# Context mixer and routing ahead of the latent stream's filters, in a two-layer hybrid diffusion kernel

## The chip, the cores and the metric

The kernel runs on one core of one Trainium2 chip. The metric is device microseconds (us) of one execution, lower is better. Its engines here are TensorE (PE in the rows), VectorE (DVE), ScalarE (ACT), GpSimd (POOL) and SyncE (SP), which issues the plain transfers. Each engine works through one list of instructions that is fixed when the kernel is built.

## The reference

Two layers work on 512 latent tokens of width 1024 and on 256 context tokens. In short form:

```
for l in range(2):
    mod_x, mod_c = silu(c) @ w_mod[l] + b_mod[l], silu(c_ctx) @ w_mod[l] + b_mod[l]   # 6 parts each
    hx, hc = rmsnorm(x)*(1+sc1)+sh1, rmsnorm(ctx)*(1+csc1)+csh1
    yx, yc = token_mixer(hx, hc)          # RG-LRU | latent attention | Hyena, one w_in before, one w_out behind
    x   = x + g1*yx
    x   = x + g2*peer(rmsnorm(x)*(1+sc2)+sh2)
    if l == 0:
        ctx = ctx + cg1*yc
        ctx = ctx + cg2*peer(rmsnorm(ctx)*(1+csc2)+csh2)
return rmsnorm(x)

def peer(h):                               # 8 heads, 16 of 128*128 experts per head and token
    s1, s2 = scores of the two halves of h @ wq against 128 keys each
    eid, gate = the 16 best sums of pairs, softmax of their scores
    return sum over the 128 (gate * gelu(h . u_tab[eid])) * v_tab[eid]
```

The Hyena convolution needs the spectra of its filters, which come from a small network (the filters) and depend on the layer's weights and the length alone, not on the tokens. The latent stream needs the context's keys, values and recurrent end state in each layer.

## The kernel before

All arithmetic is fp32; the large products are three fp32r passes over a high and a low part (`split` makes them, L113 on ACT and L114 on DVE; `mm` at L121 multiplies).

`peer` is done in two ways. For most latent tokens the tables are streamed whole, 128 blocks of `u` and of `v` (tiles `uv`, `uvh`, `uvl`, products `pst` and `dacc`; function `peer_x`). For the 256 context tokens and the last 128 latent tokens of layer 0 the rows are gathered: `gtile_u` and `gtile_v` take a tile of 128 tokens and issue 128 indirect transfers each, one row of a table per token (L1097 on POOL, tile `grow`, five buffers, 512 KB per transfer). Behind each gather stands one DVE instruction that uses it (L1108 for `u`, L1121 for `v`). Layer 0 has six such passes, 768 gathers; layer 1 has 384.

What sets the order: `schedule` is written with levels (`prio`). A lower level goes ahead, and an instruction of a higher level is put into the lists where the planner sees room. The gathers have level 6, the last. The context part has level 1, the latent mixer of layer 0 level 3. A pool gives its memory back when it closes, and what opens there afterwards waits for its tiles.

Before the change, one block at level 1 holds, in this order: the filters of the context length, the modulation's parts 0 and 1, the context's `front` (w_in, convolutions, Hyena, RG-LRU), the latent stream's filters of layer 0 (`filters`, L331 to L407), the modulation's parts 2 to 5, the context's `back` (attention, w_out), the latent stream's filters of layer 1, and parts 0 and 1 of layer 1's modulation. All its pools close there. Then comes the context's `route` (`ppq` for h @ wq, `top16` on DVE, `experts` for `eid`), still at level 1. The latent mixer's `front` of layer 0 opens its pools behind the block and not behind the routing, so that it can stand among the routing's instructions. Its products are `pwin` of 128x512 (`split=False`: 288 matmuls). The gathers of the first context tile can begin when the first half of `eid` (L1068) is there.

SP's list is in order as well: it holds the loads of the filters' transforms (`ffr`, `ffi`, L394 and L395, two buffers each), of the modulation's weights (`wmod`, L264), of `w_in`, of the routing's weights (`wpq`, L294) and others.

Of the kernel before, what the change touches and what calls it, by code (L numbers as in the profile page):

```python
# [23 lines left out]
LC = 256  # L24
# [47 lines left out]
class Kern:  # L72
# [100 lines left out]
    def schedule(self):  # L173
        a = self.a
        with ExitStack() as er:
            ec = ExitStack()
            self.context(ec, 0)
            with self.banks("ctx0", "right", w=2, S=1) as ps, ExitStack() as e0:
                md = e0.enter_context(self.pool("mod", side="right"))
                pm = e0.enter_context(self.banks("mod", "right", w=1))  # L180
                fl = e0.enter_context(self.pool("flt"))
                pf = e0.enter_context(self.banks("flt", "left", w=2, S=1))
                with self.prio(1), ExitStack() as e:
                    self.filters(fl, pf, 0, LC)
                    self.modulation(md, pm, 0, 0, 2)
                    st = self.front(e, ps, ps, 0, 1, 1, side="right")
                    self.filters(fl, pf, 0, LX)
                    self.modulation(md, pm, 0, 2, 6)
                    self.back(ps, ps, 0, 1, st, None)
                    self.filters(fl, pf, 1, LX)  # L190
                    self.modulation(md, pm, 1, 0, 2)
            self.gp = er.enter_context(self.pool("gath", side="right"))
            with self.prio(1), self.banks("rc", "right", w=2) as ps:
                gc = self.route(ps, 0, 1, "GG", side="right")
            with self.banks("x0", "left", w=2, S=2) as ps:
                with ExitStack() as e:
                    with self.prio(3):
                        pr = e.enter_context(self.banks("x0b", "right", w=2))
                        st = self.front(e, ps, pr, 0, 0, 3, split=False)
                        ex = ExitStack()  # L200
                        self.back(ps, pr, 0, 0, st, ex)
                ec.close()
            with self.prio(6):
                self.gtile_u(0, gc[0])
                self.gtile_v(0, 1, 0, gc[0])
                self.gtile_u(0, gc[1])
            with self.prio(3):
                gx, ex = self.peer_x(0, 384, 6, 32, 32, (36, 46, 46), ex)
            with self.prio(6):
                self.gtile_u(0, gx[3])  # L210
                self.gtile_v(0, 0, 3, gx[3])
                self.gtile_v(0, 1, 1, gc[1])
            with ExitStack() as ec, ExitStack() as e:
                self.context(ec, 1)
                ps = e.enter_context(self.banks("x1", "left", w=2, S=2))
                pr = e.enter_context(self.banks("x1b", "right", w=2))
                with self.prio(3):
                    st = self.front(e, ps, pr, 1, 0, 4, ctx=True)
                with self.prio(4):
                    self.back(ps, pr, 1, 0, st, None, (2, 6))  # L220
            with self.prio(5):
                gx, _ = self.peer_x(1, 320, 0, 32, 46, (44, 42, 42), ex)
            with self.prio(6):
                for i in sorted(gx, reverse=True):
                    self.gtile_u(1, gx[i])
                    self.gtile_v(1, 0, i, gx[i])
# [1211 lines left out]
```

## Time and profile before

| what | us |
|---|---|
| three runs | 4273.55, 4275.73, 4280.51 (median 4275.73) |
| the profiled execution | 4275.16 |
| its span, first to last instruction | 4273.3 |
| PE, DVE, ACT, POOL busy in it | 3707.9, 3510.8, 1904.1, 1532.1 |

The span falls into stages. Up to 318 us runs the context mixer with the filters; at 374 the first `ppq` product of its routing starts; the routing's last `eid` is there at about 531; the latent mixer's Hyena starts at about 605; at 893 the latent stream's own routing begins, with the dense `u` blocks beside it; from 1230 to 2461 the dense blocks run; at 2500 layer 1's mixer is under way. Layer 1 takes the rest. A row with a window gives, after the window and its length, each engine's busy time and in brackets its instructions, then the granted TensorE clock as a share of 2.4 GHz, the share of the 16 DMA engines that is busy, and GB/s.

### The profile page before, as it was taken

To read this page: it belongs to the slowest core of one execution; us is meant where nothing else is said; L and a number is where in the kernel's file an instruction comes from. 1 tells how busy PE (TensorE), PEld (TensorE's weight loads), DVE (VectorE), ACT (ScalarE), POOL (GpSimd) and SP (SyncE) were. 2 spreads that over 40 slices of the span, in tenths; PEclk is the share of its full clock that TensorE was granted. 3 is DMA by queue.
4 is the path that set the end of the run, shared out by engine and by line. 5 is a ranking of instruction groups with operands and counts; after the bars stand their busy time and mean duration, and the time that the engine had idled before them with its cause. 6 is when DMAs were issued, how large, how long until landed. Compare 5 with 4: busy or idle time off the path is not lost.

```text
span 4273.3 us, 63792 instructions
## 1 busy us (share of the span) xinstructions
PE 3707.9 (87%) x22514; PEld 2805.8 (66%) x22514; DVE 3510.8 (82%) x7449; ACT 1904.1 (45%) x3719; POOL 1532.1 (36%) x1225
## 2 busy tenths in 40 slices
PE   6887987968978989999969978888888999999997
PEld 3545544558878877877646656447878877776654
DVE  5746988889889889988898875755898998898988
ACT  5544243433257426622552244533334655555632
POOL 0000245642344563366436620000126345553243
PEclk7998998988999999999989989898999999999998
DMA  6654587885767897799879952242459788887697
GB/s 208 211 192 157 202 304 252 286 299 187 257 224 258 311 348 254 249 359 352 286 233 346 342 190 82 92 134 100 136 180 352 265 300 299 287 302 277 226 349 269
DMA packets 305635, 1063.74 MB, mean 249 GB/s; under 512 B 35757, under 2 KB 42625, under 8 KB 305315
## 3 DMA queue, kind: packets, MB, share of 16 engines
q0 software_dynamic: 165888, 604.05, 40.6%
q1 hardware_dynamic: 139426, 455.61, 30.6%
q8 instruction: 177, 2.90, 0.3%
q14 instruction: 144, 1.17, 0.1%
HBM read 1042.69 MB, written 16.84 MB: 248 GB/s over the span
## 4 chain that ended last, share of the span: by engine, by line
PE 32%; DMA 22%; DVE 17%; issue 16%; POOL 7%; ACT 5%; SPq 0%; POOLq 0%; DVEq 0%; ACTq 0%
PE pst L121 7%; POOL grow L1097 7%; DMA grow<-in_peer_v_dram,eid 6%; PE dacc L121 6%; DMA grow<-in_peer_u_dram,eid 6%; DMA uv<-in_peer_ut_dram 4%; PE pwin L121 4%; PE ppq L121 3%; DMA uv<-in_peer_v_dram 3%; DVE uvl L114 3%; DVE acc L1108 2%; DVE acc L1121 2%; PE pwo L121 2%; DMA wmod<-in_w_mod_dram 1%; ACT uvh L113 1%
## 5 line engine op out<-in xcount | busy, mean ns | idle before, releaser
L1097 POOL DMA_INDIRECT grow<-in_peer_u_dram,eid x576 | 747.8, 1298 | 1157.3 <-DVE acc L1108 566.4
L1097 POOL DMA_INDIRECT grow<-in_peer_v_dram,eid x576 | 776.6, 1348 | 746.4 <-DVE acc L1121 601.0
L121 PE MATMUL pst<-dhT,uvh 128*128 128x384 f32 (+1 forms) x4096 | 1001.6, 329 | 0.0
L113 ACT CAST uvh<-uv 128x1024 fp32r<-128x1024 f32 x491 | 513.0, 1045 | 680.5 <-DMA uv<-in_peer_v_dram 411.3
L121 PE MATMUL pst<-dhT,uvl 128*128 128x384 f32 (+1 forms) x2048 | 696.8, 340 | 112.3 <-DVE uvl L114 77.2
L1121 DVE SCALAR_TENSOR_TENSOR acc<-grow,gate,acc 128x1024 f32<-128x1024 f32 x571 | 732.2, 1282 | 53.8 <-DMA grow<-in_peer_v_dram,eid 46.0
L1108 DVE SCALAR_TENSOR_TENSOR acc<-grow,ghx 128x1024 f32<-128x1024 f32 x576 | 704.1, 1222 | 75.3 <-DMA grow<-in_peer_u_dram,eid 68.1
L121 PEld LDWEIGHTS pst<-dhT,uvh 128*128 128x128 f32 x4096 | 733.0, 193 | 4.1 <-issue 1.9
L114 DVE TENSOR_TENSOR uvl<-uv,uvh 128x1024 fp32r<-128x1024 f32 x491 | 599.1, 1222 | 159.5 <-ACT uvh L113 152.9
L121 PEld LDWEIGHTS pst<-dhT,uvl 128*128 128x128 f32 x2048 | 395.8, 193 | 212.3 <-DVE uvl L114 155.5
L121 PE MATMUL dacc<-uvh,wl 128*128 128x512 f32 x1154 | 481.2, 417 | 38.4 <-DVE wl L114 19.1
L121 PE MATMUL dacc<-uvl,wh 128*128 128x512 f32 x1154 | 467.3, 405 | 25.2 <-DVE uvl L114 25.1
L121 PE MATMUL dacc<-uvh,wh 128*128 128x512 f32 x1154 | 462.8, 401 | 0.0
L1235 ACT ACTIVATE o<-iota,di2n 128x128 f16<-128x128 f32 x1056 | 325.6, 390 | 28.8 <-PE pwt L1239 28.5
L121 PEld LDWEIGHTS dacc<-uvh,wl 128*128 128x128 f32 x1154 | 220.3, 191 | 128.4 <-ACT uvh L113 30.6
L121 PEld LDWEIGHTS dacc<-uvl,wh 128*128 128x128 f32 x1154 | 220.6, 191 | 82.7 <-DVE uvl L114 38.3
L121 PEld LDWEIGHTS dacc<-uvh,wh 128*128 128x128 f32 x1154 | 220.8, 191 | 48.3
L1239 PEld LDWEIGHTS <-o 128*128 128x128 f16 x4224 | 126.1, 97 | 110.7 <-issue 32.7
L1239 PE MATMUL pwt<-og,o 128*128 128x46 f16 (+3 forms) x4224 | 152.0, 182 | 43.3 <-DVE og L1225 35.5
L1205 ACT ACTIVATE PA<-pst 128x384 f32<-128x384 f32 (+1 forms) x128 | 59.5, 464 | 281.0 <-PE pst L121 280.9
L1205 ACT ACTIVATE PB<-pst 128x384 f32<-128x384 f32 (+1 forms) x128 | 59.2, 462 | 232.4 <-PE pst L121 231.8
L254 POOL MEMSET rmod<- 128x512 f32 (+1 forms) x8 | 3.3, 417 | 420.3 <-PE lpg L722 99.7
(399 smaller groups left out, 6092.6 us busy)
## 6 DMA issues: line engine op xcount, KB each, us to landing
uv<-in_peer_ut_dram SPq DMA_DIRECT2D x256, 512.0 KB
uv<-in_peer_v_dram SPq DMA_DIRECT2D x256, 512.0 KB
wmod<-in_w_mod_dram SPq DMA_DIRECT2D x96, 512.0 KB
wpq<-in_peer_wq_dram SPq DMA_DIRECT2D x48, 512.0 KB
w_in<-in_w_in_dram SPq DMA_DIRECT2D x72, 256.0 KB
w_in<-in_w_in_dram SPq DMA_DIRECT2D x18, 512.0 KB
grow<-in_peer_u_dram,eid POOLq DMA_INDIRECT x576
grow<-in_peer_v_dram,eid POOLq DMA_INDIRECT x576
```

The costliest lines, as they stand in the source:

```text
L113: self.nc.scalar.copy(hi, src)
L114: self.nc.vector.tensor_tensor(lo, src, hi.bitcast(F32), op=ALU.subtract)
L121: self.nc.tensor.matmul(p, w[i], x[j], start=start and n == 0, stop=stop and n == len(passes) - 1)
L254: nc.gpsimd.memset(r, 0.0)
L1097: self.nc.gpsimd.indirect_dma_start(out=r, out_offset=None, in_=self.a[table], in_offset=bass.IndirectOffsetOnAxis(ap=eid[:, j:j + 1], axi ...
L1108: nc.vector.scalar_tensor_tensor(junk, r, 1.0, hx, op0=ALU.mult, op1=ALU.mult, accum_out=dot[:, j:j + 1])
L1121: nc.vector.scalar_tensor_tensor(acc, r, w[:, j:j + 1], acc, op0=ALU.mult, op1=ALU.add)
L1205: nc.scalar.activation(slot(i), p, AF.Gelu_apprx_tanh)
L1235: nc.scalar.activation(o2[:, q], self.iota, AF.Abs, bias=i2n[:, t, k * NC + q:k * NC + q + 1])
L1239: nc.tensor.matmul(p[:, q, :], o2[:, q, :], og[:, g, q, :], start=(g == 0), stop=(g == 1))
```

## The change

The modulation's and the filters' pools now stand outside, on the left side, and stay open through the routing. The latent stream's filters of both layers and layer 1's modulation move behind the routing in the text and go down to level 2; the context's `back` and `route` stay at level 1. The gather's pool (`gath`) opens inside. The latent mixer's pools open when the filters' pools have closed, so behind the routing and the filters. Lines below L200 keep their numbers; those behind are 2 higher after the change.

```diff
-            with self.banks("ctx0", "right", w=2, S=1) as ps, ExitStack() as e0:
-                md = e0.enter_context(self.pool("mod", side="right"))
-                pm = e0.enter_context(self.banks("mod", "right", w=1))
+            with ExitStack() as e0:
+                md = e0.enter_context(self.pool("mod"))
+                pm = e0.enter_context(self.banks("mod", w=1))
                 fl = e0.enter_context(self.pool("flt"))
                 pf = e0.enter_context(self.banks("flt", "left", w=2, S=1))
-                with self.prio(1), ExitStack() as e:
-                    self.filters(fl, pf, 0, LC)
-                    self.modulation(md, pm, 0, 0, 2)
-                    st = self.front(e, ps, ps, 0, 1, 1, side="right")
+                with self.prio(1):
+                    with self.banks("ctx0", "right", w=2, S=1) as ps, ExitStack() as e:
+                        self.filters(fl, pf, 0, LC)
+                        self.modulation(md, pm, 0, 0, 2)
+                        st = self.front(e, ps, ps, 0, 1, 1, side="right")
+                        self.modulation(md, pm, 0, 2, 6)
+                        self.back(ps, ps, 0, 1, st, None)
+                    self.gp = er.enter_context(self.pool("gath", side="right"))
+                    with self.banks("rc", "right", w=2) as ps:
+                        gc = self.route(ps, 0, 1, "GG", side="right")
+                with self.prio(2):
                     self.filters(fl, pf, 0, LX)
-                    self.modulation(md, pm, 0, 2, 6)
-                    self.back(ps, ps, 0, 1, st, None)
                     self.filters(fl, pf, 1, LX)
                     self.modulation(md, pm, 1, 0, 2)
-            self.gp = er.enter_context(self.pool("gath", side="right"))
-            with self.prio(1), self.banks("rc", "right", w=2) as ps:
-                gc = self.route(ps, 0, 1, "GG", side="right")
```

What it does to the lists is seen at three places. The first is POOL's list before the change, over the second half of the latent mixer's `front` of layer 0 (`upad` is the padded input of a convolution, `grow` a gather):

```order
L507 MEMSET upad 128x1
L508 MEMSET upad 128x1
L1097 DMA grow<-in_peer_u_dram,eid 128x1024 x5
L492 MEMSET upad 128x2
L493 MEMSET upad 128x1
L1097 DMA grow<-in_peer_u_dram,eid 128x1024 x3
L492 MEMSET upad 128x2
L493 MEMSET upad 128x1
L1097 DMA grow<-in_peer_u_dram,eid 128x1024 x7
L492 MEMSET upad 128x2
L493 MEMSET upad 128x1
L1097 DMA grow<-in_peer_u_dram,eid 128x1024 x104
```

With 9 ahead of the first row, 24 gathers stand ahead of the last `upad`. The same list after the change, from its first gather on:

```order
L1099 DMA grow<-in_peer_u_dram,eid 128x1024 x36
L509 MEMSET upad 128x1
L510 MEMSET upad 128x1
L509 MEMSET upad 128x1
L510 MEMSET upad 128x1
L1099 DMA grow<-in_peer_u_dram,eid 128x1024 x24
L509 MEMSET upad 128x1
L510 MEMSET upad 128x1
L1099 DMA grow<-in_peer_u_dram,eid 128x1024 x4
L509 MEMSET upad 128x1
L510 MEMSET upad 128x1
L1099 DMA grow<-in_peer_u_dram,eid 128x1024 x5
```

Four groups of 4, 4, 5 and 5 follow between the other `upad`s, so that 87 gathers stand ahead of the last one, and the first 36 ahead of the first.

The second place is DVE's list where the context's routing ends. Before, the last `eid` stands among the latent convolutions (`xx`) and the start of its RG-LRU (`sp`):

```order
L555 SCALAR_TENSOR_TENSOR xx_4398<-upad,cols,xx_4398 128x512
L553 TENSOR_SCALAR xx_4399<-upad,cols 128x512
L1108 SCALAR_TENSOR_TENSOR acc,dot<-grow,ghx 128x1024
L1068 TENSOR_SCALAR eid<-pkb 128x64
L555 SCALAR_TENSOR_TENSOR xx_4399<-upad,cols,xx_4399 128x512
L685 TENSOR_SCALAR sp_5096<-cols 128x6
L703 TENSOR_SCALAR sphb<-cols 128x6
```

After the change the last `eid` (L1070) is followed by the second half of layer 1's filters (`frs`, `fkt`, `fks`), with one gather's instruction (L1110) between them each time, and the first latent norm (`xn`) stands 60 rows further down:

```order
L1070 TENSOR_SCALAR eid<-pkb 128x64
L373 TENSOR_TENSOR fsq<-fsq 128x512
L687 TENSOR_SCALAR sp_5096<-cols 128x6
L705 TENSOR_SCALAR sphb<-cols 128x6 x2
L688 TENSOR_TENSOR sp_5092<-cols,sp_5096 128x6
L1110 SCALAR_TENSOR_TENSOR acc,dot<-grow,ghx 128x1024
L690 TENSOR_SCALAR sp_5093<-sp_5092 128x6
L1110 SCALAR_TENSOR_TENSOR acc,dot<-grow,ghx 128x1024
L691 RECIPROCAL sp_5093<-sp_5093 128x6
L1110 SCALAR_TENSOR_TENSOR acc,dot<-grow,ghx 128x1024
L377 RECIPROCAL frs<-frs 128x512
L692 TENSOR_TENSOR sp_5093<-sp_5093,sp_5092 128x6
```

So the latent `front` no longer overlaps the routing; the filters do.

The third place is DVE's list at the end of layer 0 (`dacc` is the dense sum, `xs` the new latent tokens). Before, gathers of `v` go on past it:

```order
L114 TENSOR_TENSOR uvl<-uv,uvh 128x1024
L1121 SCALAR_TENSOR_TENSOR acc<-grow,gate,acc 128x1024 x3
L1304 TENSOR_TENSOR PA<-dacc_10704,PA 128x1024
L1304 TENSOR_TENSOR PA<-dacc_10705,PA 128x1024
L1146 TENSOR_TENSOR xs<-PA 128x1024 x2
L1304 TENSOR_TENSOR PA<-dacc_10706,PA 128x1024
L1121 SCALAR_TENSOR_TENSOR acc<-grow,gate,acc 128x1024
L1146 TENSOR_TENSOR xs<-PA 128x1024
L1121 SCALAR_TENSOR_TENSOR acc<-grow,gate,acc 128x1024
```

After, none is left there:

```order
L114 TENSOR_TENSOR uvl<-uv,uvh 128x1024
L1306 TENSOR_TENSOR PA<-dacc_10704,PA 128x1024
L1306 TENSOR_TENSOR PA<-dacc_10705,PA 128x1024
L1148 TENSOR_TENSOR xs<-PA 128x1024 x2
L1306 TENSOR_TENSOR PA<-dacc_10706,PA 128x1024
L1148 TENSOR_TENSOR xs<-PA 128x1024
L105 TENSOR_SCALAR nrm<-nss 128x1 x2
```

Counted over DVE's whole list, the gathers that stand ahead of five marks of layer 0 are, before and after: the routing's last `eid` 20 and 16; the latent Hyena's first product 56 and 132; the split of the latent stream's normed tokens (`dhT`) 179 and 255; the first weights of the dense part (L1220) 267 and 353; the first dense sum (L1304) 749 and 768. Between the last two marks the gathers stand equally dense against the dense blocks (`uvl`) in both lists, up to block 213 of 235; the last 22 blocks have 64 gathers before and none after.

## Rows read from the trace of the kernel before

**Rows 1.** The page: the span, and the chain that ended last by engine.

```profile
span 4273.3 us, 63792 instructions
...
PE 32%; DMA 22%; DVE 17%; issue 16%; POOL 7%; ACT 5%; SPq 0%; POOLq 0%; DVEq 0%; ACTq 0%
```

**Rows 2.** Windows by stage: length, busy us (instructions) per engine, clock, DMA.

```profile
0.00:318.00 318.00, 255.67 (x1429) 147.94 (x1430) 183.05 (x408) 162.99 (x331) 3.77 (x31) 0.89 0.61 204
318.00:374.00 56.00, 35.87 (x168) 19.29 (x167) 35.34 (x69) 28.43 (x61) 0.00 (x0) 0.75 0.55 190
374.00:531.00 157.00, 143.68 (x845) 97.95 (x845) 133.57 (x594) 57.23 (x140) 28.91 (x38) 0.97 0.51 175
531.00:605.00 74.00, 67.59 (x149) 27.89 (x148) 66.35 (x128) 40.13 (x60) 43.94 (x33) 0.95 0.82 294
605.00:893.00 288.00, 229.60 (x927) 127.94 (x926) 239.06 (x382) 95.06 (x187) 156.81 (x126) 0.87 0.82 283
893.00:1230.00 337.00, 277.90 (x1868) 264.44 (x1867) 307.83 (x1114) 122.31 (x240) 112.33 (x89) 0.90 0.62 216
1230.00:2461.00 1231.00, 1100.02 (x6888) 897.00 (x6887) 1091.63 (x1691) 549.13 (x1065) 649.54 (x482) 0.97 0.86 305
2461.00:2500.00 39.00, 9.30 (x35) 6.87 (x35) 38.86 (x62) 22.01 (x50) 19.27 (x20) 0.57 0.88 306
```

**Rows 3.** Windows of POOL's gathers alone (tile grow): length, busy us (gathers), clock, DMA.

```profile
374.00:531.00 157.00, 27.97 (x24) 0.97 0.51 175
531.00:605.00 74.00, 43.94 (x33) 0.95 0.82 294
605.00:893.00 288.00, 156.81 (x126) 0.87 0.82 283
893.00:1230.00 337.00, 112.33 (x89) 0.90 0.62 216
1230.00:2461.00 1231.00, 649.54 (x482) 0.97 0.86 305
```

**Rows 4.** The chain that ended last, by line, from 531 to 700 us.

```profile
by line: issue 49.2%; DMA grow<-in_peer_u_dram,eid 24.4%; POOL grow L1097 20.2%; DVE acc L1108 2.9%; DVE xx L555 1.2%; DVE lg L738 1.1%; POOLq L1097 0.3%; DVE sp L695 0.1%; DVE sp L694 0.1%; DVE eid L1068 0.1%; DVE sp L692 0.1%; DVE sp L689
```

**Rows 5.** The chain by line, from 60 to 318 us.

```profile
by line: PE fp L412 12.8%; PE pwo L121 10.9%; DMA w_in<-in_w_in_dram 8.6%; PE pwin L121 7.1%; DMA wmod<-in_w_mod_dram 6.6%; issue 4.2%; DMA gw<-in_lru_g_dram 3.7%; PE bps L833 3.3%; PE pmod L266 3.2%; PE hpf L412 2.9%; PE lpg L722 2.7%; PE 
```

**Rows 6.** SP's waits, 318 to 380 us: us in total, times, longest.

```profile
SPq L394 <- PE fp L412: 16.8, 2, 15.7
SPq L395 <- PE fp L412: 6.8, 3, 2.8
```

**Rows 7.** DVE groups by shape, 0 to 365 us: count, busy us, mean ns, idle before.

```profile
L375 DVE RECIPROCAL frs<-frs 128x512 f32<-128x512 f32 x6 | 20.1, 3352 | 6.5 <-ACT frs L374 6.5
...
L378 DVE TENSOR_TENSOR fkt<-fkt,frs 128x512 f32<-128x512 f32 x20 | 13.2, 683 | 0.1
...
L380 DVE TENSOR_TENSOR fks<-fkt 128x1024 f32<-128x1024 f32 x4 | 4.8, 1210 | 0.0
```

**Rows 8.** DVE groups, 374 to 893 us.

```profile
L1108 DVE SCALAR_TENSOR_TENSOR acc<-grow,ghx 128x1024 f32<-128x1024 f32 x128 | 156.4, 1222 | 20.3 <-DMA grow<-in_peer_u_dram,eid 19.1
...
L555 DVE SCALAR_TENSOR_TENSOR hc<-upad,cols,hc 128x512 f32<-128x512 f32 x12 | 9.0, 750 | 0.0
```

**Rows 9.** PE in order of time: start, us, matmuls of the latent front.

```profile
426.64 11.32 PE L121 MATMUL pwin<-hT,w_in 128*128 128x512 f32 x26
```

**Rows 10.** Windows of POOL's gathers alone, two stretches.

```profile
800.00:850.00 50.00, 33.93 (x27) 1.00 0.89 313
1900.00:1950.00 50.00, 33.96 (x25) 0.97 0.97 360
```

**Rows 11.** Windows of all engines, dense blocks with few and with many gathers.

```profile
1700.00:1790.00 90.00, 89.01 (x758) 75.61 (x757) 85.85 (x178) 63.55 (x139) 29.39 (x23) 1.00 0.70 234
2320.00:2456.00 136.00, 124.16 (x462) 85.51 (x460) 115.27 (x109) 32.66 (x44) 83.22 (x62) 1.00 0.94 344
```

**Rows 12.** The page's group of POOL's gathers of u, whole span.

```profile
L1097 POOL DMA_INDIRECT grow<-in_peer_u_dram,eid x576 | 747.8, 1298 | 1157.3 <-DVE acc L1108 566.4
```

## The prediction

> **What bounds the kernel now.** I read the page first, then windows by stage, then the chain and the waits inside the early stages, and last the lists of the two kernels. The page's chain changes engine all the time: no engine holds more than 32% of it, and a sixth is "issue" [rows 1]. So the whole-span busy shares say little, and I go by stage. Up to 318 us the context mixer and the filters run with DVE busy 183 of 318 us; then come 56 us to the first routing product, 157 us of routing with the latent `front` beside it (PE 144 of 157), 74 us to the latent Hyena, 288 us to the latent routing, and 337 and 1231 us in which DVE and PE are both near 90% [rows 2]. Layer 1 has the same lists in both kernels and is left out.
>
> Two things in these rows carry the argument. First, from the context's routing on the gathers are in the way: between 531 and 700 us the chain is almost wholly the gather's loop (issue 49%, transfer 24%, POOL 20%) [rows 4]. A gather has no slack there, since DVE's list is in order: the latent mixer's instructions stand behind the instruction that uses a gathered row, and that one stands behind the transfer. Second, the loop has a pace. Its best stretch has 27 gathers in 50 us, 1.85 us each; beside a steady stream of other loads it has 25, 2.0 us each [rows 10]; in the latent Hyena and attention 126 in 288, 2.3 us each [rows 3]. What DVE alone pays is 1.22 us [rows 8].
>
> **The change part by part.** No arithmetic is removed or added. What moves is order, so each term below is a stage's new length less its old one; the gathers ahead of each mark are the counts given with the change.
>
> *Up to the first routing product (374 us): -43.* On the chain from 60 to 318 us the filters' products `fp` hold 12.8% of 258, 33 us [rows 5]. Of the 136 filter matmuls that stand ahead of the first `ppq` in PE's list, 77 move behind it, 57%; 57% of 33 is 19. After 318 us SP's list, with `wpq` in it, waits 16.8 + 6.8 = 24 us for `fp` to free transform buffers [rows 6]. The sum is -43. Bounds: -57 if all of both goes; -10 if the loads of `wmod` and `w_in`, 15% of that chain, which stay ahead, take over what the filters leave. I take -43, since both pieces have rows.
>
> *The context's routing (157 us): +8.* DVE was busy 133.6 us in it [rows 2]. Out go 24 latent convolution steps at 0.75 [rows 8], 18 us, and 4 gathers, 5 us. In come the filters: 59 of their 132 DVE instructions stand behind the first `wpq` split, 12 rescalings at 0.683, 12 sums and differences at about 1.21, 3 reciprocals at 3.35 [rows 7], together 33, and 32 small ones that I put at 0.5 (their nearest row is 0.683), 16: 49 us. Some 12 of it come behind the last `eid`, so 37 stand here. 133.6 - 18 - 5 + 37 = 148. DVE's share was 0.85 there; PE, 144 of 157 us busy, loses the latent products, so I take 0.90: 165 us, +8. At 0.85 it is 174 (+17), at 0.95 156 (-1).
>
> *From the last `eid` to the latent Hyena (74 us): +150.* This is the largest term. Before, the latent `front` was two thirds done here, and 56 - 20 = 36 gathers passed. Now the whole `front` comes behind the last `eid`, behind the filters' end, with 132 - 16 = 116 gathers between its instructions. Its products need 288 x 11.32/26 = 125 us of PE [rows 9], so PE doesn't bound it. DVE's work: 116 x 1.22 = 142, the stage's other work before 66 - 36 x 1.22 = 22, the convolutions from the routing 18, the filters' end 12, norms and splits about 10: 204. The gathers' pace gives 116 x 1.85 = 215 to 116 x 2.0 = 232, and 2.3 would be 267. I take the middle of the two good paces, 224, +150; ends +141 and +193. The cover that the old order had, PE-heavy products beside DVE-heavy sorting, is what is given up; what comes in its place, filters beside sorting, wants DVE twice.
>
> *The latent Hyena and attention (288 us): 0.* The same work with 255 - 132 = 179 - 56 = 123 gathers among it. At a pace of 2.0 it would be 246, -42; nothing in its lists changes, so I take 0.
>
> *The latent routing (337 us): +12.* 353 - 255 = 98 gathers pass instead of 88, in a stage where DVE is busy 308 of 337 us [rows 2]: 10 x 1.22, all of it on DVE's path.
>
> *The dense blocks (1231 us): -10.* Here a naive count would give the gain: 415 gathers instead of 482. But up to block 213 the lists are equally dense, so the pace of the blocks is the same. Only the last 22 blocks are free of gathers. Before, that stretch (136 us) has PE at 0.91; a stretch with few gathers has 0.99 [rows 11]. 136 x (1 - 0.91/0.99) is about 10 us. Ends 0 and -15.
>
> *The step to layer 1 (39 us): -20.* DVE is busy 38.9 of 39 us there [rows 2], and the gathers behind the last dense sum, 768 - 749 = 19 by the list, of which 16 lie in this window, go: 16 x 1.22. Ends -10 and -25.
>
> Sum: -43 + 8 + 150 + 0 + 12 - 10 - 20 = +97. The profiled execution took 4275.2 us, of which 4273.3 are span, and lies 0.6 under the median; 4275.2 + 97 = 4372 us. As a cross-check, DVE has 183 + 35 + 134 + 66 + 239 = 657 busy us in the first 893 [rows 2], a share of 0.74; with 76 more gathers, 93 us, the same share gives 1019, 126 later, against 115 from the terms.
>
> A page of the Trainium skill speaks against the pace I use. "DMA: Bandwidth & Descriptors", section "Anatomy of one DMA — SWDGE (gpsimd) path", puts a transfer issued by GpSimd at about 2.0 us plus its bytes over 436 GB/s. For 512 KB that is an estimate of 3.2 us, so five buffers would never hold the loop, and the big stage would be bound by DVE's 204 us: the sum would be about 20 lower, 4352. The rows above show 1.85 to 2.3 us per gather, and I go by them.
>
> **The rivals.**
>
> *The early stages lose their waits: faster.* The first gather comes earlier, and DVE is idle 236 of the first 893 us; the gathers could fill that. It takes the context part to lose `fp` (33), the loads on its chain (15% of 258, 39) and SP's 24, -96; the routing at -1; the big stage at 1.85, +141; the Hyena stage at 2.0, -42. Then the latent routing begins 2 us later than before, and 2 + 12 - 10 - 20 = -16: 4259 us. For it speak the idle DVE and 27 gathers in 50 us; against it, that those loads stay in SP's list and that no early stage had DVE above 0.90. It decides when the first `ppq` product starts before about 285 us and the latent Hyena by about 650. Chance 0.10.
>
> *The order changes and the time doesn't.* The lost overlap is given back by the earlier gathers, with the terms somewhere between that rival and my own low end (-57 - 1 + 141 - 42 + 12 - 10 - 20 = +23). That needs three terms at their ends at once. Within 0.2%, 4267 to 4284 us, which is about what a measurement of this kernel tells from no change: chance 0.06.
>
> *The gathers run at the slow pace: slower still.* If the big stage has the pace of the Hyena stage, 2.3 us, because the latent weights' loads (18 x 512 KB of `w_in`, then `w_out`) meet the gathers, its term is +193: 4415 us; with the context part at -10 too, 4448. For it speaks that 33 and 126 gathers took 74 and 288 us [rows 3], neither at 2.0; against it the 1.85 of one stretch. Chance 0.20. The Trainium skill has a rule on its side, "SBUF — State Buffer", section "Who interferes with whom": a DVE instruction with two SBUF inputs shuts out a GpSimd instruction that reads SBUF until it ends. By that a gather's 1.3 us on POOL [rows 12] would follow DVE's 1.22 us each time, an estimate of 2.5 us, and the big stage would be 290 us long, 4438. The 27 in 50 us show that this doesn't hold each time.
>
> *That the gathers don't start earlier at all*, since `eid` still waits for the same sorting, is the first term at its upper end, and lies in the range.
>
> **How the numbers follow.** My forecast has 0.64, with its own range 4298 to 4415. Slower by over 0.2%: 0.64 + 0.20 = 0.84; within: 0.06; faster: 0.10. The time is that of the forecast. Its lower end must take in part of what lies between it and the faster rival, its upper end most of the slow pace: 4272 to 4430 leaves out about 0.10 below and 0.06 above.
>
> **What would show it.** Right: the first `ppq` product near 331 us, the last `eid` near 496, the latent Hyena near 720, the first `dhT` split near 1008; 1240 us or so from the first L1222 weights to layer 1's step, with the last blocks at PE 0.99 and no gather in the step; layer 1 as long as before. Wrong: a Hyena that starts by 650, since then the `front` isn't held by the gathers; or dense blocks that run faster from their first block on, since then a gather costs more there than the density of the lists tells.

## The result, and the profile after

The changed kernel takes 4385.74 us (median of 6 runs, 4370.09 to 4391.81) against 4273.21 us for the kernel before, run beside it: a ratio of 1.0265, 95% interval 1.0246 to 1.0283. It is slower, by 113 us; forecast were 97 and the range 4272 to 4430 holds it. The profiled execution has a span of 4389.9 us, 116.6 more than before [rows 1], and the sums below go by it.

The first lines of the page: span, busy time of each engine, and the chain that ended last.

```profile
span 4389.9 us, 63803 instructions
...
PE 3740.3 (85%) x22514; PEld 2828.6 (64%) x22514; DVE 3515.2 (80%) x7449; ACT 1896.2 (43%) x3714; POOL 1532.5 (35%) x1225
...
PE 34%; DMA 22%; DVE 17%; issue 15%; POOL 6%; ACT 6%; SPq 0%; POOLq 0%; DVEq 0%; ACTq 0%
```

The same mix of engines as before. The answer lies in the stages. The windows of the kernel after (length, busy us of PE, PE's weight load, DVE, ACT and POOL, granted clock, DMA share, GB/s) answer to [rows 2], but for two places: the context and the wait behind it are one row here, and the stretch from the last `eid` to the latent Hyena has two halves:

```profile
0.00:323.00 323.00, 252.80 (x1428) 143.25 (x1428) 169.66 (x404) 150.16 (x318) 3.55 (x27) 0.87 0.62 207
323.00:494.00 171.00, 116.86 (x764) 93.74 (x765) 141.92 (x589) 65.72 (x148) 20.55 (x20) 0.79 0.40 141
494.00:571.00 77.00, 25.78 (x84) 15.44 (x82) 60.17 (x136) 21.39 (x51) 47.43 (x37) 0.57 0.78 280
571.00:747.00 176.00, 145.62 (x318) 62.54 (x317) 138.55 (x226) 48.95 (x74) 99.09 (x96) 0.90 0.90 327
747.00:1035.00 288.00, 224.68 (x928) 126.41 (x926) 243.99 (x304) 92.17 (x186) 152.78 (x124) 0.88 0.80 272
1035.00:1384.00 349.00, 284.77 (x1858) 270.21 (x1857) 313.18 (x1206) 119.49 (x236) 129.83 (x99) 0.87 0.63 218
1384.00:2594.00 1210.00, 1096.04 (x6884) 895.36 (x6882) 1017.16 (x1542) 549.49 (x1066) 560.85 (x415) 0.97 0.80 282
2594.00:2622.00 28.00, 11.65 (x46) 8.36 (x44) 20.41 (x43) 20.80 (x49) 0.00 (x0) 0.63 0.25 85
```

What the reader is to see: 74 us [rows 2] have become 77 + 176. In the first of the two, PE is busy a third of the time, while DVE and POOL work through gathers. Marks taken from both traces, with the forecast of each step (us; a stage's change is its new length less its old one; the latent Hyena's mark is its first spectral multiplication on DVE, some 14 us behind the end of the window in the rows):

| mark | before | after | the stage ahead of it | forecast |
|---|---|---|---|---|
| first `ppq` | 373.7 | 323.4 | -50 | -43 |
| last context `eid` | 530.8 | 494.4 | +14 | +8 |
| latent Hyena | 618.6 | 760.7 | +178 | +150 |
| first `dhT` split | 893.5 | 1034.7 | -1 | 0 |
| first dense weights | 1228.7 | 1383.7 | +14 | +12 |
| first dense sum | 2460.6 | 2594.2 | -21 | -10 |
| layer 1's first `pwin` | 2497.9 | 2621.7 | -10 | -20 |
| end | 4273.3 | 4389.9 | -7 | 0 |

All of the loss is the third line. Its middle, on PE in order of time (start, us, instruction, idle time before and what ended it), and then DVE at the same place:

```profile
529.40 2.08 PE L414 MATMUL fp<-fab,ffi 128*128 128x256 f32 x4 [2.30 <-DMA ffi<-in_fwd_dram]
548.47 1.97 PE L441 MATMUL ptr<-ident,xn 128*128 128x128 f32 x8 [17.00 <-DVE nrm L105]
...
570.71 9.88 PE L121 MATMUL pwin<-hT,w_in 128*128 128x512 f32 x19 [1.09 <-DVE hT L454]
```

```profile
538.20 1.23 DVE L1110 SCALAR_TENSOR_TENSOR acc<-grow,ghx 128x1024 f32<-128x1024 f32 x1 [0.79 <-DMA grow<-in_peer_u_dram,eid]
539.36 0.08 DVE L1110 DVE_READ_ACCUMULATOR acc<-grow,ghx 128x1 f32 x1
544.79 1.23 DVE L1110 SCALAR_TENSOR_TENSOR acc<-grow,ghx 128x1024 f32<-128x1024 f32 x1 [5.35 <-DMA grow<-in_peer_u_dram,eid]
545.94 0.08 DVE L1110 DVE_READ_ACCUMULATOR acc<-grow,ghx 128x1 f32 x1
545.94 0.15 DVE L105 TENSOR_SCALAR nrm<-nss 128x1 f32<-128x1 f32 x1
```

The last product of layer 1's filters ends at 531.5. Only behind it does the latent `front` begin: in SP's list its first load (`xr`) goes out right behind the filters' last store (`spec`), at 532.9 us.

```profile
523.73 9.13 SPq L409 DMA_DIRECT2D spec<-fst  x3
532.92 0.96 SPq L434 DMA_DIRECT2D xr<-in_x_dram  x2
```

Then comes the norm of its first rows: ACT has the sum of squares by 541 us. The 0.15 us of `nrm` that PE's transposes need stand in DVE's list behind an instruction that waits 5.35 us for a gathered row, so PE resumes at 548.5. On DVE such waits add up, in the stretch from 494 to 760 us (us in total, times, longest), to

```profile
DVE acc L1110 <- DMA grow<-in_peer_u_dram,eid: 46.8, 38, 5.4
```

and POOL's gathers of the two halves (length, busy us and count, clock, DMA share, GB/s) come at 77/33 = 2.3 us and 176/82 = 2.15 us:

```profile
494.00:571.00 77.00, 47.16 (x33) 0.57 0.78 280
571.00:747.00 176.00, 98.16 (x82) 0.90 0.90 327
```

The chain by line from 494 to 760 us answers to [rows 4]; the gather's loop (issue, transfer, POOL) still has 81% of it:

```profile
by line: issue 34.0%; DMA grow<-in_peer_u_dram,eid 30.5%; POOL grow L1099 16.3%; DMA spec<-fst 5.1%; DVE acc L1110 4.6%; DMA grow<-in_peer_v_dram,eid 3.9%; DMA xr<-in_x_dram 2.7%; DVE hc L557 1.6%; DVE acc L1123 0.5%; DVE xn L423 0.5%; ACT 
```

By that line the gathers look like the whole cause. The experiments say otherwise.

### The profile page after: what moved, and what is told of

Same layout as the page of the kernel before. It is cut to its first block, busy times and chain, and to the rows that moved or that the text cites. A ratio compares the mean times of both kernels' runs of the same rounds, so it can differ in the third digit from the quotient of the medians.

```text
span 4389.9 us, 63803 instructions
## 1 busy us (share of the span) xinstructions
PE 3740.3 (85%) x22514; PEld 2828.6 (64%) x22514; DVE 3515.2 (80%) x7449; ACT 1896.2 (43%) x3714; POOL 1532.5 (35%) x1225
## 4 chain that ended last, share of the span: by engine, by line
PE 34%; DMA 22%; DVE 17%; issue 15%; POOL 6%; ACT 6%; SPq 0%; POOLq 0%; DVEq 0%; ACTq 0%
PE dacc L121 9%; PE pst L121 7%; DMA grow<-in_peer_u_dram,eid 7%; POOL grow L1099 6%; DMA uv<-in_peer_ut_dram 5%; DMA grow<-in_peer_v_dram,eid 4%; PE pwin L121 3%; DMA uv<-in_peer_v_dram 3%; PE ppq L121 3%; DVE uvl L114 2%; DVE acc L1110 2%; DVE acc L1123 2%; PE pwo L121 1%; ACT uvh L113 1%; DMA wmod<-in_w_mod_dram 1%
## 5 line engine op out<-in xcount | busy, mean ns | idle before, releaser
L1110 DVE SCALAR_TENSOR_TENSOR acc<-grow,ghx 128x1024 f32<-128x1024 f32 x576 | 704.3, 1223 | 104.1 <-DMA grow<-in_peer_u_dram,eid 98.6
L121 PE MATMUL pwin<-hT,w_inh 128*128 128x256 f32 (+1 forms) x576 | 146.2, 345 | 0.1
```

Of the source, the lines that this page charges most:

```text
L121: self.nc.tensor.matmul(p, w[i], x[j], start=start and n == 0, stop=stop and n == len(passes) - 1)
L1110: nc.vector.scalar_tensor_tensor(junk, r, 1.0, hx, op0=ALU.mult, op1=ALU.mult, accum_out=dot[:, j:j + 1])
```

## The experiments

"A set" is the latent filters of one layer, `filters(l, LX)`. Code is cut at "...". The theories at the start: the front was put behind the filters and behind the gathers (mine), or the pools that stay open are what it waits for.

**Pools alone.** The text order and the level of before, with the nesting of after.

```
-            with self.banks("ctx0", "right", w=2, S=1) as ps, ExitStack() as e0:
-                md = e0.enter_context(self.pool("mod", side="right"))
+            with ExitStack() as e0:
+                md = e0.enter_context(self.pool("mod"))
...      (routing inside e0; filters and modulation where before has them)
```

> The filters and the modulation stand where the kernel before has them, but their pools lie on the left and stay open through the routing, as in the changed kernel. In its lists no gather stands ahead of the latent front's first convolution and 71 ahead of the 21st product of a Hyena (the latent one's fifth), 67 in the kernel before and 143 in the changed one. Theory 1 (the loss comes from the latent front being put behind the last filters and behind the gathers): the latent front lies beside the routing again; latent Hyena near 619 us in the trace, end 4275 us (4250 to 4300). Theory 2 (the loss comes from the pools that stay open, whose memory the latent front must wait for): the latent front starts as late as in the changed kernel, latent Hyena near 760 us, end 4385 us (4360 to 4410).

Measured: 4283.66 against 4272.72 us, ratio 1.003 (1.0016 to 1.0043). The latent front starts at 418 us (408 before), the latent Hyena comes at 636. The pools cost some 13 us (7 to 18 by the interval); they are not the 113.

**Gathers held back.** The changed kernel, and its context indices pass through a copy that follows the last latent projection:

```
                         st = self.front(e, ps, pr, 0, 0, 3, split=False)
+                        gc = {i: self.held(gc[i], st["cq"][2][:, 0:1]) for i in gc}
...
+    def held(self, g, src):
+        hx, eid, gate, n = g
+        new = self.gp.tile([128, 128], I32, name="eid", bufs=3)
+        self.nc.vector.tensor_copy(new[:, 0:1], src)
+        self.nc.vector.tensor_copy(new, eid)
+        return hx, new, gate, n
```

> The changed kernel, with the context's indices copied once more, by a copy that must follow the latent front's last projection; so no gather of them can start before it. Some 10 gathers stand ahead of the latent Hyena's fifth product (143 in the changed kernel), 122 ahead of the first dhT split (255). Theory 1a (the gathers in the list are what the latent front waits on): the stretch from the last eid to the latent Hyena falls from 266 us towards what PE needs, 172 us busy, so 200 us (180 to 220), latent Hyena near 695 us. Theory 1b (the front is held by the filters' tail and is bound by PE and its weights; gathers lie in gaps that are there anyway): latent Hyena stays at 750 us (735 to 770). The 133 gathers then fall to the later stages: DVE is busy 1017 of 1210 us in the dense blocks, so 133 x 1.29 = 172 us more would fill it. Under 1a the end comes between 4330 and 4400 us (4365), by how much of them the dense blocks hide; under 1b 4390 to 4450 us.

Measured: 4398.9 us, ratio 1.0288 (1.0259 to 1.0316): nothing gained. But the marks moved as theory 1a has it: from the last `eid` to the latent Hyena it takes 199 us, not 266, and the Hyena comes at 694. The end lies at the upper end of that theory's range. Windows of this run, the two halves of the stretch, the latent routing with the dense blocks, the step and layer 1's first part:

```profile
495.00:543.00 48.00, 26.23 (x74) 16.31 (x74) 17.76 (x62) 19.54 (x48) 0.26 (x4) 0.58 0.32 110
543.00:694.00 151.00, 148.19 (x355) 66.60 (x356) 55.36 (x74) 52.69 (x80) 0.93 (x14) 0.99 0.32 103
...
968.00:2531.00 1563.00, 1381.27 (x8757) 1163.22 (x8755) 1397.74 (x2814) 670.67 (x1306) 764.44 (x571) 0.95 0.81 286
2531.00:2568.00 37.00, 8.05 (x32) 6.13 (x32) 36.87 (x59) 20.92 (x49) 20.01 (x21) 0.53 0.89 303
2568.00:3067.00 499.00, 389.89 (x1913) 258.19 (x1914) 312.53 (x535) 176.27 (x333) 77.84 (x79) 0.89 0.45 150
```

Two things follow. Without a gather the stretch is still 199 us: 48 until the front's first product (the set's last copy is at 519 us, 24 in), then 151 with PE busy for 148. PE's products of the front among them (matmuls, busy us, mean ns, idle before):

```profile
L121 PE MATMUL pwin<-hT,w_in 128*128 128x512 f32 x288 | 126.6, 599 | 0.6 <-DVE hT L455 0.6
```

So 111 of the 178 us are the filters' tail and the serial front, and only 67 the gathers. And the gathers held back return. The latent routing and the dense blocks, taken together, hide theirs (61 more in 4 us more), but 55 land in layer 1's front and 17 in its step, where after has none. The rows of after for those two stretches:

```profile
1035.00:2594.00 1559.00, 1380.82 (x8740) 1165.57 (x8738) 1330.34 (x2746) 668.97 (x1300) 690.68 (x514) 0.95 0.76 267
2622.00:3057.00 435.00, 384.32 (x1915) 256.07 (x1915) 238.06 (x474) 174.85 (x332) 2.81 (x24) 0.94 0.32 101
```

Layer 1's front takes 499 against 435 us, the step 37 against 28. That is 73 us for 72 gathers; a gather pushed past the dense blocks costs 1 us of the end. (POOL's counts in the rows take in a few other instructions; the gathers are counted by their tile.)

**One part: layer 1's set and the modulation behind the routing, layer 0's set at its old place.**

```
                         st = self.front(e, ps, ps, 0, 1, 1, side="right")
+                        self.filters(fl, pf, 0, LX)
...
                 with self.prio(2):
-                    self.filters(fl, pf, 0, LX)
                     self.filters(fl, pf, 1, LX)
```

> One part of the change alone: the latent filters of layer 0 stand at their place of before, those of layer 1 and the second layer's modulation behind the routing. In the lists 10 gathers stand ahead of the latent front's first convolution (0 before, 55 in the changed kernel) and 89 ahead of the latent Hyena's fifth product (67 before, 143 changed). Theory 1 (place of the latent front and gathers ahead of it): the loss goes with the 22 more gathers, 22 x 1.9 = 42 us, less some 10 us since the routing's first weight loads stand behind 18 and not 20 of the filters' loads: end 4305 us (4280 to 4335), latent Hyena near 650 us. Theory 2 (the open pools): 4385 us (4360 to 4410). Theory 3 (layer 1's filters behind the routing are the whole loss, wherever layer 0's stand): also near 4385 us.

Measured: 4271.96 us, ratio 0.9999 (0.9987 to 1.0012). All three theories expected a loss and there is none. In the trace layer 1's set, though written behind the routing, still runs beside the context: its last column sum `fsum` starts at 342 us (332 before, 495 after). Its first product comes at 237 us, as before, 5 us behind the last copy of layer 0's set; in after the two come at 371 and 372. So the later text and the lower level didn't hold it back here. The first `ppq` comes 30 us earlier, the latent Hyena 26 later, and the stages behind give it back. So what counts is when a set runs, not where it is written. And putting layer 0's set back is enough to undo the whole loss, with the pools still open and the modulation still written behind the routing.

**Layer 1's set behind the latent mixer.**

```
-                    self.filters(fl, pf, 1, LX)
-                    self.modulation(md, pm, 1, 0, 2)
...
+            with self.prio(3), ExitStack() as e1:     # behind x0
...      (pools of its own, opened here)
+                self.filters(fl, pf, 1, LX)
+                self.modulation(md, pm, 1, 0, 2)
```

> The changed kernel without layer 1's filters and its modulation in front of the latent front: they stand behind the latent mixer, in pools of their own. Pools stay open through the routing as in the changed kernel. In the lists 7 gathers stand ahead of the latent front's first convolution and 84 ahead of the latent Hyena's fifth product (67 before, 143 changed). Theory 1: the routing starts as early as in the changed kernel (first ppq near 323 us, 374 before), the latent front lies beside it again, and the latent Hyena starts near 600 us (560 to 630); layer 1's filters then take some 60 us of PE behind or beside the latent mixer; end 4270 us (4220 to 4310). Theory 2 (open pools): latent Hyena near 740 us, end 4385 us.

Measured: 4390.03 us, ratio 1.0284 (1.0258 to 1.0309). Theory 1 is right up to the latent Hyena (622 us, 619 before, 761 after) and wrong at the end: the stretch from there to the first `dhT` split is 407 us, 275 before. The set runs from 892 to 1025 us, and the split comes at 1029.6.

```profile
622.00:1029.00 407.00, 281.08 (x1132) 143.92 (x1132) 329.50 (x462) 120.26 (x230) 221.43 (x174) 0.78 0.81 282
```

The loss went with the set. Against the changed kernel without the set at all (below) it is 3.2%, 138 us, the modulation's move included. This is where my theory fell: the latent front's place is not the cause but the first victim. The new theory, A: a set away from the context mixer costs about what it lasts, whatever has to wait for it. Its rival, B: a set costs its PE work anywhere.

**Level alone**, with before's pools closed ahead of the routing: both sets and the modulation at level 2.

```
-                    self.filters(fl, pf, 0, LX)
                     self.modulation(md, pm, 0, 2, 6)
+                    with self.prio(2):
+                        self.filters(fl, pf, 0, LX)
                     self.back(ps, ps, 0, 1, st, None)
-                    self.filters(fl, pf, 1, LX)
-                    self.modulation(md, pm, 1, 0, 2)
+                    with self.prio(2):
+                        self.filters(fl, pf, 1, LX)
+                        self.modulation(md, pm, 1, 0, 2)
```

> The pools nested as in the kernel before (closed ahead of the routing), but the latent filters and the second layer's modulation at level 2, so behind the context mixer in the priorities. In the lists 27 gathers stand ahead of the latent front's first convolution (0 before, 55 changed), 115 ahead of the latent Hyena's fifth product (67 and 143), 226 ahead of the first dhT split (179 and 255). Theory A (what costs is that layer 0's filters leave the context mixer's gaps, which two sets share nearly free; the pools matter little): some two thirds of the loss, end 4345 us (4320 to 4385), latent Hyena near 715 us. Theory B (level and open pools are both needed for the loss): 4275 us (4260 to 4295).

Measured: 4364.17 us, ratio 1.0218 (1.019 to 1.0246). Most of the loss is there with the pools closed ahead of the routing, inside theory A's range. Layer 0's first `fsum` is at 243 us, as in after (242); the latent Hyena comes at 733.

**The price of layer 1's set, after and before.** In both kernels the set is left out, and layer 1 reads layer 0's spectra.

```
-                    self.filters(fl, pf, 1, LX)
...
-                    nc.sync.dma_start(kk, self.spec[l, L][m, :, o].rearrange("p a c -> p (a c)"))
+                    nc.sync.dma_start(kk, self.spec[0, L][m, :, o].rearrange("p a c -> p (a c)"))
```

> The changed kernel without layer 1's filters at all; layer 1's Hyena reads layer 0's spectra, so a whole set of filters is left out. Theory A (a set of filters that doesn't stand beside the context mixer costs what it lasts, about 130 us, since the latent front or the latent mixer then waits for it): first ppq near 323 us, latent Hyena near 620, first dhT near 895, end 4255 us (4235 to 4275). Theory B (a set costs its PE work, 60 to 75 us, wherever it stands): latent Hyena near 690, end 4320 us (4300 to 4335).

> The kernel before without layer 1's filters, in the same way as in the changed one: what a set costs at its old place. Theory A (beside the context mixer it stands in gaps that are there anyway, and costs the 24 us in which SP waits for it and a little more): end 4240 us (4215 to 4260), so that the two kernels without this set lie within 30 us of each other, where with it they lie 115 apart. Theory B (it costs its PE work, 60 to 75 us, here too): end 4205 us (4190 to 4220), and the gap between the two kernels stays near 115 us.

Measured: 4255.74 us (ratio 0.9962, 0.9945 to 0.9978) and 4209.24 us (0.9856, 0.9829 to 0.9883). In after the set costs 1.0265 - 0.9962 = 3.0%, 129 us: A. In before it costs 1.44%, 61 us: B's number, so "nearly free beside the context" was wrong. The two kernels without it lie 46 us apart, which neither theory had (within 30, or still 115): with this set left out, 68 of the 113 us are gone. Stage windows of after without the set, and of before without it, from the last `eid` to the latent Hyena:

```profile
482.00:618.00 136.00, 112.09 (x264) 48.90 (x262) 111.68 (x197) 42.41 (x68) 68.05 (x63) 0.94 0.85 315
```

```profile
494.00:576.00 82.00, 74.03 (x175) 32.46 (x174) 72.83 (x134) 44.93 (x67) 40.80 (x33) 0.96 0.81 289
```

Both are free of PE's dead stretch (clock 0.94 and 0.96). What is left between them is how much of the front was done beside the routing: its first `pwin` comes at 416 and at 356 us.

**The set in a third place**, the step to layer 1 (the kernel before; pools of its own, level 4).

```
-                    self.filters(fl, pf, 1, LX)
-                    self.modulation(md, pm, 1, 0, 2)
...
+            with self.prio(4), ExitStack() as e1:     # behind the dense blocks
...      (pools of its own, opened here)
+                self.filters(fl, pf, 1, LX)
+                self.modulation(md, pm, 1, 0, 2)
```

> The kernel before, with layer 1's filters and the second layer's first modulation parts behind the dense blocks, in the step to layer 1, in pools of their own. Without the set the kernel before took 4209 us. Theory A (a set that has no other work beside it costs its whole length, some 135 us as in the changed kernel): latent Hyena near 575 us, first dense sum near 2395, then layer 1's first projection some 140 us behind it; end 4345 us (4310 to 4380). Theory B (a set costs its PE work, 60 to 75 us, wherever it stands, and what the changed kernel pays more has to do with the latent front alone): end 4275 us (4255 to 4295).

Measured: 4341.21 us, ratio 1.0156 (1.0134 to 1.0178): A's number. Against the kernel without the set it is 3.0%, 128 us, the modulation's move included. The step takes 162 us, 37 before:

```profile
2407.00:2569.00 162.00, 70.00 (x276) 31.33 (x276) 98.53 (x136) 48.70 (x97) 30.53 (x31) 0.60 0.56 204
```

PE is busy for 70 of 162 us. The waits of that window (us in total, times, longest) go round the engines, and the modulation's loads add theirs:

```profile
ACT fh L325 <- DVE farg L324: 32.9, 2, 19.2
...
PE pmod L271 <- DMA wmod<-in_w_mod_dram: 28.9, 8, 14.2
...
ACT fst L406 <- PE fp L417: 22.5, 7, 7.0
PE fp L417 <- ACT fab L391: 21.3, 2, 11.0
ACT fab L391 <- DVE fab L388: 20.5, 2, 10.6
```

DVE for the sine's argument, ACT for the sine, PE for the product, ACT and DVE for `fab`, PE for `fp`, ACT for its copy: a set is one chain over three engines, and its links wait for one another. The largest of these waits is not the chain's own, though. In the first half of the set, up to its first `fsum` at 2477 us, DVE's list still holds the tail of the gathers, and the short steps of `farg` stand between them; their instructions alone (tile `grow`, DVE) are 31 of the 57 us:

```profile
2420.00:2477.00 57.00, 30.68 (x25) 0.56 0.99 379
```

The set's last copy ends at 2545.4, and layer 1's front begins behind it. Its first norm waits for the set's last store, on ACT and on DVE:

```profile
2546.15 1.06 ACT L424 ACTIVATE xn<-xs 128x1024 f32<-128x1024 f32 x1 [0.74 <-DMA spec<-fst]
...
2548.13 0.15 DVE L105 TENSOR_SCALAR nrm<-nss 128x1 f32<-128x1 f32 x1 [12.85 <-DMA spec<-fst]
```

**Layer 0's set back, layer 1's left out**: the changed kernel without the set, plus the first edit of the one-part run.

> The changed kernel without layer 1's filters (a set left out; layer 1 reads layer 0's spectra) and with layer 0's latent filters back at their place of before, beside the context mixer; pools open through the routing as in the changed kernel. Without layer 1's set the changed kernel took 4256 and the kernel before 4209 us. Theory A1 (that gap of 46 us is the place of layer 0's set): 4215 us (4200 to 4230), latent Hyena near 585 us. Theory A2 (it is the open pools and the modulation behind the routing): stays near 4255 us (4240 to 4270), latent Hyena near 618.

Measured: 4231.69 us, ratio 0.989 (0.9864 to 0.9916). Between both theories, nearer A1: of the 1.06% between the two kernels without layer 1's set, 0.72% (31 us) is layer 0's place and 0.34% (15 us) is left for the open pools and the modulation. That last figure is not resolved by itself here. The run with the pools alone has 13 us, but in the one-part run pools and modulation stood as they do here and the time was that of before.

**Candidates.** If a set is best hosted by the context mixer, put it there for good. The first: layer 1's set directly behind layer 0's in the kernel before.

```
                     self.filters(fl, pf, 0, LX)
+                    self.filters(fl, pf, 1, LX)
                     self.modulation(md, pm, 0, 2, 6)
                     self.back(ps, ps, 0, 1, st, None)
-                    self.filters(fl, pf, 1, LX)
```

> A candidate to beat both: the kernel before with layer 1's filters directly behind layer 0's, ahead of the context's last modulation parts and its back half, so that the context mixer hosts both sets and the filters' loads no longer stand around the routing's first weights. In the lists no gather stands ahead of the latent front's first convolution and 60 ahead of the latent Hyena's fifth product (67 before). Theory A: the first ppq falls from 374 towards 350 us, if the context mixer itself isn't held up by the earlier filters; end 4255 us (4230 to 4280). Theory B (DVE and PE are both full there, so the filters hold up the context by what they no longer hold up later): 4273 us (4262 to 4290).

Measured: 4253.76 us, ratio 0.9962 (0.9947 to 0.9978): faster than both kernels, by 16 us than before. Against the kernel without the set that is a price of 1.06%, 45 us, and the set is through in 83 us (238 to 322), where at its old place it took 127. Not for the reason given: the first `ppq` comes later (379 us), since the context ends 41 us later. The latent front, though, starts at 391, not 408 us, and from the `dhT` split to the first dense sum it takes 12 us less; the last is not explained. Two further steps the same way undo it: with the modulation moved along (`self.modulation(md, pm, 1, 0, 2)` behind the set), and with both sets one place earlier (layer 0's ahead of the context's `front`, layer 1's behind it).

> A candidate: layer 1's filters and the second layer's modulation directly behind layer 0's latent filters, ahead of the context's last modulation parts; the run with the filters alone there took 0.996 of the time before. If what helps is that the latent front starts earlier (391 against 408 us) since the filters' pool closes earlier, this one gains as much, 4254 us (4240 to 4265); if the earlier loads of the modulation hold up the context's, it is back at 4272 us (4262 to 4285).

> A candidate: both latent sets one place earlier still, layer 0's ahead of the context's front and layer 1's directly behind it. By the theory that early sets stand in gaps of the context mixer this is worth as much as the early set alone, 4254 us (4235 to 4265); if the sets now stand ahead of the context's own instructions, the context ends some 40 us later and the time is 4290 us (4272 to 4310).

Measured: 1.0003 (0.9986 to 1.0021) and 1.0025 (1.0007 to 1.0043). There the context ends at 367 and 377 us (356 in the first candidate), and the first `ppq` comes at 392 and 402 us (379 in the first candidate).

## Why the prediction was right, and where it wasn't

The sign, the stage and the size were right; of the largest term the mechanism was half right.

*First `ppq`, -43:* -50. The context ends 21 us earlier (19 forecast for `fp`), and the wait from there to the first product is 29 us shorter (24 forecast).

*Routing, +8:* +14, inside its bounds. DVE is busy 142 us (148 forecast). Its share is 0.83, about the 0.85 of before; 0.90 was the step too much.

*Last `eid` to latent Hyena, +150:* +178. The sentence that failed is "so PE doesn't bound it". The forecast had one loop of 116 gathers fill 224 us. With the gathers held, the stretch is 199 us: the filters' tail and then PE, whose 288 `pwin` products took 126.6 us, the 125 of the prediction. These stand in a row, the norms and transposes between, and the gathers slow both by 67. Pace and PE each explain 200 us or more alone, so that the total came out near is partly luck and didn't show which one ruled. The loop of the gathers did run at 2.15 to 2.3 us, near the slow rival's pace.

A sentence of the Trainium skill was weighed there: its page "DMA: Bandwidth & Descriptors", section "Anatomy of one DMA — SWDGE (gpsimd) path", gave an estimate of 3.2 us for a gather. The profile's median from issue to landing is 6.6 us, over the whole span:

```profile
grow<-in_peer_u_dram,eid POOLq DMA_INDIRECT x576, 6.6
```

and DVE waits for it 38 times in that stretch. By the Trainium skill's figure the stretch would have been 20 us shorter than forecast; it was longer, and the trace decides.

*Hyena and attention, 0; latent routing, +12:* -1 and +14.

*Dense blocks, -10:* -21. Up to block 213 the pace is the same (1085.7 and 1082.7 us from block 30), as the prediction had it; the last 22 take 116 instead of 136 us:

```profile
2471.00:2587.00 116.00, 116.00 (x449) 84.56 (x449) 44.60 (x50) 33.30 (x46) 0.00 (x0) 1.00 0.39 136
```

PE's share is 1.00, as expected, but its busy time itself fell, from 124.2 [rows 11] to 116.0. A term made of shares couldn't hold that.

*Step, -20:* -10. The gathers are gone, but the step's other work, DVE 20 and ACT 21 of the 28 us that stay, was beneath them. *Layer 1, 0:* -7, not explained.

*The cause behind the terms* was not in the prediction: it priced what waits for the filters, never the filters. What the runs show is one row of steps, each behind the last (first product to last copy of a set, and the latent front's first norm, in us):

| kernel | layer 0's set | layer 1's set | front's first norm | ratio |
|---|---|---|---|---|
| before | 74 to 234 | 237 to 364 | 369 | 1 |
| after | 201 to 372 | 371 to 532 | 540 | 1.0265 |
| level alone | 200 to 355 | 354 to 498 | 506 | 1.0218 |
| one part (layer 0's set back) | 73 to 232 | 237 to 390 | 398 | 0.9999 |
| after without layer 1's set | 203 to 360 | none | 367 | 0.9962 |

Layer 1's set starts when layer 0's is through, and the front's first norm comes 5 to 8 us behind the last copy of the last set. So the move of layer 0's set is enough for the loss. With layer 1's set left out, 68 of the 113 us are gone, 31 more go with layer 0's place, and some 15 stay for the pools and the modulation; but that split holds for this order of steps alone, since layer 0's set put back by itself takes all of the 113.

The rival "faster" counted on early gathers being worth something. They are: the held gathers cost 1 us each at the end. It fell because the filters' tail and the serial front alone, without a gather, make the stretch 111 us longer; the gathers in front of them add 67.

## What to carry to other kernels

What a chain of small dependent steps over several engines costs depends on what waits for its end. The same set cost 61 us at its old place in the context mixer, 45 a little earlier there, and 128 to 138 in three other places (in two of them with the modulation), where a front or a routing could start only when it was through. In the changed kernel it even had company, since for most of its life it ran beside the context's routing. No run puts a set elsewhere without something behind it, nor gives what follows memory of its own, so how much is the waiting for its pools and how much the want of a neighbour stays open.

So before moving such a block, ask what will start only behind it and which other chain runs beside it there, and read its start and end from the trace, since a low level in the text may change nothing. A chain of waits that is full of one operation shows what was last, not what would be left without it: here the gathers' loop had 81% of the chain, holding the gathers back took 67 of 178 us off that stretch, and nothing off the whole.

## What had not been expected of the hardware

The granted clock in the dead stretch was 0.57, near the lower of TensorE's two levels (1.2 of 2.4 GHz), with PE busy 26 of 77 us, and 0.58 with the gathers held (26 of 48 us); 0.60 in the step that held the set. It was 0.50 from 545 to 571 us, behind PE's 17 us of waiting for `nrm`. So PE's work in such a gap is dearer too: the front's transposes took 426 ns each in the dead stretch, and 272 ns in the kernel before without layer 1's set, at a clock of 0.98.

```profile
545.00:571.00 26.00, 8.09 (x33) 6.57 (x34) 21.77 (x54) 11.58 (x30) 16.86 (x13) 0.50 0.87 300
L441 PE MATMUL ptr<-ident,xn 128*128 128x128 f32 x32 | 7.8, 426 | 30.4 <-DVE nrm L105 17.0 <-DVE nry L106 7.0 <-DVE xn L423 6.3
...
344.00:494.00 150.00, 143.81 (x837) 95.30 (x838) 129.58 (x581) 51.17 (x123) 33.04 (x39) 0.98 0.49 173
L438 PE MATMUL ptr<-ident,xn 128*128 128x128 f32 x8 | 1.5, 272 | 0.0
```

And one gather took 2.15 us with the DMA share at 0.90, against 1.85 at 0.89 [rows 10]: the share doesn't tell the pace.
